# Gate and up of the feed-forward: half the contraction by seven block products, down products between the blocks, hidden tile turned through memory

## The chip, the cores and the metric

One core of a Trainium2 chip runs the whole program. The metric is the device time of one launch in microseconds, the median of several runs. TensorE multiplies; VectorE, ScalarE and GpSimd do the elementwise work; SyncE issues the loads of the weights.

## The reference

Two transformer layers over 256 tokens of width 2048, in float32. The mixers (sparse and linear attention in layer 0, stick-breaking attention in layer 1) are not touched. Each layer has this feed-forward, with `w_gate` and `w_up` of 2048 x 5632 and `w_down` of 5632 x 2048:

```python
xn = rmsnorm(h, norm_g)
h = h + (silu(xn @ w_gate) * (xn @ w_up)) @ w_down
```

## The kernel before

**Products.** The tokens stand in two halves of 128 (`tt`), the contraction in chunks of 128, the columns in blocks of 512. A float32 operand is split into a rounded part and a remainder (`hi`, `lo`), and a product is three passes of TensorE: hi x hi, hi x lo, lo x hi (L201 to L203). The activations, already turned and split, are `aH` and `aL` (`hH` and `hL` for the hidden tile); the row's norm factor is applied after the product.

**The stream of weights.** `unit` (L176) handles four chunks: SyncE loads 1 MB into a `raw` tile (two buffers), then for each half of two chunks ScalarE casts to `whi` (L99), VectorE subtracts to `wlo` (L100), four buffers each, and TensorE makes 2 chunks x 2 halves of tokens x 3 passes = 12 products of 512 columns. Such a half is called a half unit. `block` strings units together: 16 chunks are 8 half units, 96 products.

**The feed-forward.** The 11 blocks of hidden columns stand in groups of three (the last has two). `gate_up` makes a group: for each block the gate's 96 products, silu on ScalarE (L799), the up's 96 products, the multiplication on VectorE (L802), both halves into `sl`. Then `sl` is turned: 16 transposes on VectorE per block (L128), each turning 32 x 32 squares of a quarter of the partitions into `hx`, and a split into `hH`, `hL` (L789, L790). `down` multiplies a group's hidden tile with `w_down` in four column blocks and adds them to `h` (L234). The order is: gate and up of group 0, gate and up of group 1, all four column blocks of group 0's down, and so on.

**Order of the work.** The code is written out in one stream; the small tasks (turns, splits) wait in a list and are let in one at a time after a half unit (`later`, `tick`). A scheduler then gives every engine a fixed order, and an engine works through its order strictly, waiting where an operand is not there. A buffer is written again when its last reader is done. Products go to four PSUM tiles in turn (`mm`), transposes to four others (`at`).

Of the kernel before, what the change touches and what calls it, by code (L numbers as in the profile page):

```python
# [9 lines left out]
F32 = mybir.dt.float32  # L10
F32R = mybir.dt.float32r
# [6 lines left out]
NT = 2  # L18
# [9 lines left out]
def trunk_kernel(ctx: ExitStack, tc: tile.TileContext, x, p, even_norm, even_w_in, even_w_gk,  # L28
# [10 lines left out]
    psm = ctx.enter_context(tc.tile_pool(name="psm", bufs=4, space=bass.MemoryType.PSUM))  # L39
    pst = ctx.enter_context(tc.tile_pool(name="pst", bufs=4, space=bass.MemoryType.PSUM))  # L40

    def mm_tile():
        return psm.tile([P, NB], F32, name="mm")

    def at_tile():
        return pst.tile([P, NB], F32, name="at")

# [17 lines left out]
    # the activation tables and the tensor engine's clock are up when the data comes  # L65
# [7 lines left out]
    # norm gains, one row of 128 per chunk, turned so that a chunk's gains lie along the partitions  # L73
# [61 lines left out]
    def turn_h(dst, norm, c2):  # L135
        """Chunks 2*c2 and 2*c2+1 of h, transposed, times the gain, split."""
# [24 lines left out]
    def later(fn, key=None, delay=2, after=None):  # L161
        """fn, some half units of weights from now, and some after the work that `after` names."""
# [13 lines left out]
    def unit(ps, stat, k0, cols, first, last, nk=KU, kw0=None, step=KU, pre=None):  # L176
        """nk chunks of the contraction: cols = [(weight, first column, width)]."""
# [10 lines left out]
        for j in range(0, nk, 2):  # L188
# [794 lines left out]
```

## Time and profile before

| | |
|---|---|
| median of 3 runs | 2441.42 us (2440.93 to 2441.71) |
| the profiled execution, first to last instruction | 2438.5 us |
| TensorE, VectorE, ScalarE, GpSimd busy | 99%, 62%, 47%, 1% |
| first gate load of layer 0, last down load of layer 1 | 374.0 us, 2307.2 us |

The busy share of an engine is an average over stages. What a change is worth depends on which engine is late in its stage; for that the rows below show time lines of the feed-forward, where several engines can be laid side by side by their microseconds. A matmul's duration in the trace includes its way through the array; the distance between starts is what it costs in a stream.

### The profile page before, as it was taken

The page shows a single profiled execution, that of the slowest core. Times are in us where ns is not written, and L with a number is a line of the kernel's source. Part 1 is how long each engine was busy: PE and PEld are TensorE (multiplying, and loading weights), DVE is VectorE, ACT ScalarE, POOL GpSimd, SP SyncE. Part 2 cuts the span into 40 slices and gives each one's busy share as a digit, 9 for nine tenths or more (in the row PEclk, how much of TensorE's full clock was granted, in tenths as well). Part 3 has the DMA queues.
Part 4 walks back from the last instruction along what each step waited for, and adds up shares of the span by engine and source line. Part 5 has one row for each costly group of instructions (what it writes and reads, how often), then busy time and mean ns, then how long its engine had stood idle before and what let it go on. Part 6 is the DMA issues. An engine that isn't in the chain of part 4 may idle for free.

```text
span 2438.5 us, 27647 instructions
## 1 busy us (share of the span) xinstructions
PE 2417.6 (99%) x10966; PEld 1996.5 (82%) x10966; DVE 1506.6 (62%) x1907; ACT 1154.1 (47%) x1418; POOL 19.2 (1%) x45
## 2 busy tenths in 40 slices
PE   8999999999999999999999999999999999999998
PEld 7887788888888888888888888888888888888887
DVE  5765555766756665655676666557667556556564
ACT  6644444344434434446546565544444344444463
POOL 0000000000000000000000000000000000000000
PEclk9999999999999999999999999999999999999999
DMA  6454455566556565555554454555655655556563
GB/s 211 147 169 151 144 194 186 189 196 201 189 192 193 186 205 183 198 190 185 178 190 156 161 184 165 180 190 177 203 190 192 205 190 186 196 187 206 182 231 123
DMA packets 231651, 450.01 MB, mean 185 GB/s; under 512 B 9457, under 2 KB 16337, under 8 KB 231394
## 3 DMA queue, kind: packets, MB, share of 16 engines
q1 hardware_dynamic: 231234, 447.07, 55.6%
q8 instruction: 86, 1.41, 0.2%
q10 hardware_dynamic: 288, 1.18, 0.1%
q14 instruction: 43, 0.35, 0.0%
HBM read 446.12 MB, written 2.10 MB: 184 GB/s over the span
## 4 chain that ended last, share of the span: by engine, by line
PE 91%; issue 5%; ACT 2%; DVE 1%; DMA 1%; SPq 0%; POOLq 0%; POOL 0%; DVEq 0%; ACTq 0%
PE mm L202 29%; PE mm L201 29%; PE mm L203 29%; PE at L141 1%; DVE kT L128 1%; DVE wlo L100 0%; DMA raw<-in_odd_w_in_dram 0%; PE at L424 0%; DMA h<-in_x_dram 0%; PE at L742 0%; DVE sp L719 0%; ACT whi L99 0%; ACT sp L716 0%; ACT sp L715 0%; ACT L715 0%
## 5 line engine op out<-in xcount | busy, mean ns | idle before, releaser
L100 DVE TENSOR_TENSOR wlo<-raw,whi 128x1024 fp32r<-128x1024 f32 (+2 forms) x848 | 1020.7, 1213 | 794.1 <-ACT whi L99 790.1
L99 ACT CAST whi<-raw 128x1024 fp32r<-128x1024 f32 (+2 forms) x848 | 874.8, 1042 | 1053.5 <-PE mm L203 668.8
L201 PE MATMUL mm<-whi,aH 128*128 128x512 f32 (+2 forms) x2656 | 1036.9, 390 | 0.7 <-ACT whi L99 0.7
L202 PE MATMUL mm<-wlo,aH 128*128 128x512 f32 (+2 forms) x2656 | 1028.8, 387 | 4.1 <-DVE wlo L100 4.1
L203 PE MATMUL mm<-whi,aL 128*128 128x512 f32 (+2 forms) x2656 | 1028.7, 387 | 0.0
L202 PEld LDWEIGHTS mm<-wlo,aH 128*128 128x128 f32 x2656 | 499.4, 188 | 104.7 <-DVE wlo L100 5.9
L203 PEld LDWEIGHTS mm<-whi,aL 128*128 128x128 f32 x2656 | 499.1, 188 | 103.4 <-issue 1.0
L201 PEld LDWEIGHTS mm<-whi,aH 128*128 128x128 f32 x2656 | 499.2, 188 | 102.9 <-issue 2.8
L201 PE MATMUL mm<-whi,hH 128*128 128x512 f32 x704 | 277.2, 394 | 0.0
L202 PE MATMUL mm<-wlo,hH 128*128 128x512 f32 x704 | 277.0, 393 | 0.0
L203 PE MATMUL mm<-whi,hL 128*128 128x512 f32 x704 | 273.6, 389 | 0.0
L128 DVE STREAM_TRANSPOSE hx<-sl 32x256 f32<-32x256 f32 x352 | 153.6, 436 | 6.1
L201 PEld LDWEIGHTS mm<-whi,hH 128*128 128x128 f32 x704 | 132.2, 188 | 30.0
L203 PEld LDWEIGHTS mm<-whi,hL 128*128 128x128 f32 x704 | 132.2, 188 | 29.7
L202 PEld LDWEIGHTS mm<-wlo,hH 128*128 128x128 f32 x704 | 132.4, 188 | 26.1
L146 ACT ACTIVATE aH<-at,gT 128x256 fp32r<-128x256 f32 x96 | 45.1, 473 | 51.4 <-DVE aL L147 47.5
L789 ACT CAST hH<-hx 128x1024 fp32r<-128x1024 f32 x22 | 23.2, 1054 | 92.6 <-DVE hx L128 92.6
L147 DVE SCALAR_TENSOR_TENSOR aL<-at,gT,aH 128x256 fp32r<-128x256 f32 x96 | 45.8, 480 | 22.0 <-ACT aH L146 21.9
L234 DVE TENSOR_TENSOR h<-mm,h 128x512 f32<-128x512 f32 x80 | 52.4, 682 | 2.7 <-PE mm L203 2.7
L141 PE MATMUL at<-ident,h 128*128 128x128 f32 x192 | 30.5, 283 | 5.0 <-DMA h<-in_x_dram 5.0
L141 PEld LDWEIGHTS at<-ident,h 128*128 128x128 f32 x192 | 24.9, 145 | 11.8 <-DMA h<-in_x_dram 3.0
L128 DVE STREAM_TRANSPOSE qT<-tok 32x256 f32<-32x256 f32 x64 | 27.9, 436 | 6.8 <-ACT tok L762 5.8
(221 smaller groups left out, 806.8 us busy)
## 6 DMA issues: line engine op xcount, KB each, us to landing
raw<-in_ffn_w_gate_dram SPq DMA_DIRECT2D x88, 1024.0 KB, 5.2
raw<-in_ffn_w_up_dram SPq DMA_DIRECT2D x88, 1024.0 KB, 5.2
raw<-in_ffn_w_down_dram SPq DMA_DIRECT2D x88, 1024.0 KB, 5.0
raw<-in_odd_w_in_dram SPq DMA_DIRECT2D x48, 1024.0 KB, 5.2
raw<-in_even_w_in_dram SPq DMA_DIRECT2D x36, 1024.0 KB, 5.0
raw<-in_ple_w_gate_dram SPq DMA_DIRECT2D x28, 1024.0 KB, 5.1
raw<-in_even_w_out_dram SPq DMA_DIRECT2D x16, 1024.0 KB, 5.1
raw<-in_odd_w_out_dram SPq DMA_DIRECT2D x16, 1024.0 KB, 5.0
```

The source lines that it names most:

```text
L99: nc.scalar.copy(hi, raw)
L100: nc.vector.tensor_tensor(lo, raw, hi.bitcast(F32), OP.subtract)
L128: nc.vector.transpose(dst[32 * a:32 * a + 32, :, :, 32 * q:32 * q + 32], src.rearrange("p t (m a c) -> p t m a c", a=4, c=32)[32 * q:32 * ...
L141: nc.tensor.transpose(ps[:, c, tt, :], h[:, tt, k * P:(k + 1) * P], ident)
L146: nc.scalar.activation(dst[0][:, k, :], src, AF.Copy, scale=g)
L147: nc.vector.scalar_tensor_tensor(dst[1][:, k, :], src, g, dst[0][:, k, :].bitcast(F32), op0=OP.mult, op1=OP.subtract)
L201: nc.tensor.matmul(ps[tt][:, :n], sh, hi[:, c, :n], start=st, stop=False)
L202: nc.tensor.matmul(ps[tt][:, :n], sh, lo[:, c, :n], start=False, stop=False)
L203: nc.tensor.matmul(ps[tt][:, :n], sl, hi[:, c, :n], start=False, stop=en)
L234: nc.vector.tensor_tensor(hs, ps[tt], hs, OP.add)
L789: nc.scalar.copy(d[0], t)
```

## The change

**Seven products for eight.** Take two chunks of the contraction, the two halves of the tokens, and one block of 512 columns of gate beside the same of up: a 2 x 2 block matrix times a 2 x 2 block matrix, eight block products, each of three passes. The change makes seven products of sums (Winograd's form) from them and combines the seven results. It does so for the first eight of the 16 chunks (four *pairs*), in blocks 1 to 10; the other eight chunks go through `unit` as before (here called the plain units, four half units of gate and four of up). Block 0 stays as it was.

The sums of activations are made and split once a layer, in block 0 (`sums_of_operand`, into `sT`). The sums of weights are made on VectorE in every pair (L850 to L852, into `T`): one of 1024 elements per partition and two of 512. A pair's split goes in four pieces with 1, 2, 2 and 2 blocks of 512 columns, thus 3, 6, 6 and 6 products. The seven results lie in PSUM banks that are fixed by number; the plain units are added on top of four of them, and VectorE and ScalarE combine the banks (L876 to L880, L886) in the tile `E`. All PSUM is now one tile `bank` whose slices are handed out in turn.

**Down between the blocks.** After each block of gate and up in groups 1 to 3, one or two of the four column blocks of the group before follow.

**The turn through memory.** In place of 16 transposes and `hx`, one transpose of 32 x 32 squares over all partitions (L143), four stores to DRAM of 128 KB and two loads of 256 KB, all on GpSimd's queue (L147, L151). The cast (L904) and the subtraction (L905) of what comes back follow at least four half units later.

```diff
-    psm = ctx.enter_context(tc.tile_pool(name="psm", bufs=4, space=bass.MemoryType.PSUM))
-    pst = ctx.enter_context(tc.tile_pool(name="pst", bufs=4, space=bass.MemoryType.PSUM))
-
-    def mm_tile():
-        return psm.tile([P, NB], F32, name="mm")
-
-    def at_tile():
-        return pst.tile([P, NB], F32, name="at")
...
+    bank = psp.tile([P, 8, NB], F32, name="bank")
+    turns = {"mm": 0, "at": 0}
+
+    def mm_tile():
+        turns["mm"] += 1
+        return bank[:, (turns["mm"] - 1) % 4]
+
+    def at_tile():
+        turns["at"] += 1
+        return bank[:, 4 + (turns["at"] - 1) % 4]
...
+    def cross(src, pool):
+
+
+
+        tq = pool.tile([P, 4, NT, 4, 32], F32, name="tq", bufs=1)
+        nc.vector.transpose(tq.rearrange("p a t m r -> p t m a r"),
+                            src.rearrange("p t (m a c) -> p t m a c", a=4, c=32))
+        y = yp.tile([4, 32, 4, NT, P], F32, name="ty")
+        for q in range(4):
+            nc.gpsimd.dma_start(y[:, :, q].rearrange("a c t n -> c a (t n)"),
+                                tq[32 * q:32 * q + 32].rearrange("c a t m r -> c a (t m r)"))
+        x = pool.tile([P, NT, 4, 4, 32], F32, name="tx", bufs=1)
+        for t in range(NT):
+            nc.gpsimd.dma_start(x[:, t].rearrange("p q m r -> p q (m r)"),
+                                y[:, :, :, t].rearrange("a c q n -> (a c) q n"))
+        return x.rearrange("p t q m r -> p m (t q) r")
+
...
-                    st = first and j + c == 0
+                    st = first and tt >= begun and j + c == 0
...
+    NS = 4
+    B2, B4, B3, B22, B1, B5, B6, B7 = range(8)
+
...
+        ST = act.tile([P, 2, 4, NS, P], F32R, name="sT", tag="aH")
+        work = act.tile([P, 8, NB], F32, name="work", tag="aL")
+        T, E = work[:, 0:4], work[:, 4:8]
...
+        def product(p, stat, hi, lo, first, last):
+            for m, (a, b) in enumerate(((stat[0], hi), (stat[0], lo), (stat[1], hi))):
+                nc.tensor.matmul(bank[:, p], a, b, start=first and m == 0, stop=last and m == 2)
+
+        def pair(j, b):
+
+            raw = wp.tile([P, KU, NB], F32, name="raw", bufs=2).rearrange("p (r c) n -> p r c n", r=2)
+            for c, w in enumerate((ffn_w_gate[i], ffn_w_up[i])):
+                nc.sync.dma_start(raw[:, :, c], w[2 * j * P:(2 * j + 2) * P, b * NB:(b + 1) * NB]
+                                  .rearrange("(k q) n -> q k n", q=P))
+
+            nc.vector.tensor_tensor(T[:, 0:2], raw[:, 0], raw[:, :, 1], OP.add)
+            nc.vector.tensor_tensor(T[:, 2], T[:, 1], raw[:, 0, 0], OP.add)
+            nc.vector.tensor_tensor(T[:, 3], T[:, 2], raw[:, 1, 0], OP.add)
+
+            def tok(c, t):
+                return [x[:, 2 * j + c, t * P:(t + 1) * P] for x in xs]
+
+            def comb(n):
+                return [ST[:, hl, n, j] for hl in range(2)]
+
+            pieces = [(raw[:, 0, 0:1], [(B1, tok(0, 0))]), (T[:, 0:2], [(B5, comb(0)), (B7, comb(2))]),
+                      (T[:, 2:4], [(B6, comb(1)), (B4, tok(1, 1))]),
+                      (raw[:, 1], [(B2, tok(1, 0)), (B3, comb(3))])]
+            for n, (src, ps) in enumerate(pieces):
+                hi = wp.tile([P, 2, NB], F32R, name="whi")
+                lo = wp.tile([P, 2, NB], F32R, name="wlo")
+                split_sb(src, hi[:, :len(ps)], lo[:, :len(ps)])
+                for c, (p, stat) in enumerate(ps):
+                    product(p, stat, hi[:, c], lo[:, c], j == 0, j == NS - 1 and p >= B1)
+                if n % 2:
+                    tick()
+
+        def gate_up_7(b):
+            need(("sT", i))
+            for j in range(NS):
+                pair(j, b)
+            nc.scalar.copy(E[:, 0], bank[:, B1])
+            nc.vector.tensor_tensor(E[:, 2], bank[:, B6], E[:, 0], OP.add)
+            nc.vector.tensor_tensor(E[:, 1], bank[:, B7], E[:, 2], OP.add)
+            nc.vector.tensor_tensor(E[:, 3], bank[:, B5], E[:, 1], OP.subtract)
+            nc.vector.tensor_tensor(E[:, 2], bank[:, B5], E[:, 2], OP.subtract)
+            for n, w in enumerate((ffn_w_gate[i], ffn_w_up[i])):
+                for k in range(2 * NS, KC, KU):
+                    unit([bank[:, 2 * n], bank[:, 2 * n + 1]], xs, k, [(w, b * NB, NB)], n == 1 and k == 2 * NS,
+                         k + KU == KC, begun=1)
+                e = E[:, 2 * n:2 * n + 2]
+                nc.vector.tensor_tensor(e, bank[:, 2 * n:2 * n + 2], e, OP.add)
+                if n == 0:
+                    sl = fp.tile([P, NT, NB], F32, name="sl")
+                    for tt in range(NT):
+                        nc.scalar.activation(sl[:, tt], E[:, tt], AF.Silu, scale=rstd_of(nkey)[:, tt:tt + 1])
+            return sl, [E[:, 2 + tt] for tt in range(NT)]
+
+        def gate_up_8(b):
...
+            later(sums_of_operand, key=("sT", i))
+            return sl, block(xs, [(ffn_w_up[i], b * NB, NB)])
...
+            x = {}
+            later(lambda: x.update(x=cross(sl, fp)), key=("xT", i, b))
+            later(lambda: split_hid(hT[gi], x["x"], 4 * n), key=("hT", i, b), after=(("xT", i, b), 4))
...
+        for gi, g in enumerate(groups):
+            for n in range(len(g)):
+                gate_up(gi, n)
+                if gi:
+                    for cb in range(4 * n // len(g), 4 * (n + 1) // len(g)):
+                        down(gi - 1, cb, None)
+        nx = nx_fn()
+        for cb in range(4):
+            down(len(groups) - 1, cb, nx)
+        return nx
```

The order on VectorE before, in layer 0 behind a block of gate and up (L802 multiplies gate and up, L128 turns, L100 subtracts for the weights, L790 for the hidden tile):

```order
L802 SCALAR_TENSOR_TENSOR sl<-mm,rstd,sl 128x512 x2
L128 STREAM_TRANSPOSE hx<-sl 32x2x4x32 x8
L100 TENSOR_TENSOR wlo<-raw,whi 128x1024
L128 STREAM_TRANSPOSE hx<-sl 32x2x4x32 x4
L100 TENSOR_TENSOR wlo<-raw,whi 128x1024
L128 STREAM_TRANSPOSE hx<-sl 32x2x4x32 x4
L100 TENSOR_TENSOR wlo<-raw,whi 128x1024
L790 TENSOR_TENSOR hL<-hx,hH 128x1024
L100 TENSOR_TENSOR wlo<-raw,whi 128x1024 x13
```

And of the change, in block 4 from the end of the column block of down products that stands before it (L259 adds to `h`, L850 to L852 sum weights, L107 subtracts for the weights, L905 for the hidden tile):

```order
L259 TENSOR_TENSOR h<-bank,h 128x512 x2
L851 TENSOR_TENSOR work<-work,raw 128x512
L107 TENSOR_TENSOR wlo<-raw,whi 128x1024
L905 TENSOR_TENSOR hL<-tx,hH 128x1024
L852 TENSOR_TENSOR work<-work,raw 128x512
L107 TENSOR_TENSOR wlo<-raw,whi 128x512
L107 TENSOR_TENSOR wlo<-work,whi 128x1024 x2
L107 TENSOR_TENSOR wlo<-raw,whi 128x1024
L850 TENSOR_TENSOR work<-raw 128x1024
L107 TENSOR_TENSOR wlo<-raw,whi 128x512
L851 TENSOR_TENSOR work<-work,raw 128x512
L107 TENSOR_TENSOR wlo<-work,whi 128x1024
```

Where VectorE had one subtraction per 12 products, it now has a sum or two beside each subtraction per 6 products.

The order on ScalarE before, over a block of gate and up in layer 0 (L799 is silu, L99 casts weights, L789 the hidden tile):

```order
L799 ACTIVATE sl<-mm,rstd 128x512 x2
L99 CAST whi<-raw 128x1024 x11
L789 CAST hH<-hx 128x1024
L99 CAST whi<-raw 128x1024 x5
L799 ACTIVATE sl<-mm,rstd 128x512 x2
L99 CAST whi<-raw 128x1024 x11
```

And of the change, in the last two pairs of block 4 and behind them (L106 casts weights, L876 copies a PSUM bank to `E`, L890 is silu):

```order
L106 CAST whi<-raw 128x512
L106 CAST whi<-work 128x1024 x2
L106 CAST whi<-raw 128x1024
L106 CAST whi<-raw 128x512
L106 CAST whi<-work 128x1024
L876 COPY work<-bank 128x512
L106 CAST whi<-work 128x1024
L106 CAST whi<-raw 128x1024 x8
L890 ACTIVATE sl<-work,rstd 128x512 x2
```

The copy L876 stands between the casts of the last pair's second and third piece.

## Rows read from the trace of the kernel before

**Rows 1.** The page: span, busy time of each engine, slices of TensorE, VectorE and clock.
```profile
span 2438.5 us, 27647 instructions
...
PE 2417.6 (99%) x10966; PEld 1996.5 (82%) x10966; DVE 1506.6 (62%) x1907; ACT 1154.1 (47%) x1418; POOL 19.2 (1%) x45
...
PE   8999999999999999999999999999999999999998
...
DVE  5765555766756665655676666557667556556564
...
PEclk9999999999999999999999999999999999999999
```

**Rows 2.** Busy time by stretches of the first feed-forward.
```profile
core 0: us, PE busy (x) PEld busy (x) DVE busy (x) ACT busy (x) POOL busy (x), PEclk, DMA share, GB/s
...
580.00:680.00 100.00, 100.00 (x442) 82.58 (x441) 65.03 (x78) 43.48 (x44) 0.00 (x0) 1.00 0.61 202
680.00:780.00 100.00, 100.00 (x441) 82.52 (x440) 56.60 (x62) 39.87 (x39) 0.00 (x0) 1.00 0.58 188
780.00:880.00 100.00, 100.00 (x441) 82.58 (x440) 65.87 (x79) 42.53 (x43) 0.00 (x0) 1.00 0.60 195
```

**Rows 3.** Timeline of ScalarE in the first feed-forward: start, duration, instruction, idle before.
```profile
765.92 1.06 ACT L99 CAST whi<-raw 128x1024 fp32r<-128x1024 f32 x1 [1.66 <-PE mm L203]
...
777.69 2.00 ACT L99 CAST whi<-raw 128x1024 fp32r<-128x1024 f32 x2 [3.54 <-DMA raw<-in_ffn_w_up_dram]
```

**Rows 4.** Timeline of VectorE over the same microseconds.
```profile
759.99 1.40 DVE L802 SCALAR_TENSOR_TENSOR sl<-mm,rstd,sl 128x512 f32<-128x512 f32 x2
761.43 3.57 DVE L128 STREAM_TRANSPOSE hx<-sl 32x256 f32<-32x256 f32 x8
...
771.20 1.23 DVE L100 TENSOR_TENSOR wlo<-raw,whi 128x1024 fp32r<-128x1024 f32 x1
772.34 1.22 DVE L790 TENSOR_TENSOR hL<-hx,hH 128x1024 fp32r<-128x1024 f32 x1
773.48 2.35 DVE L100 TENSOR_TENSOR wlo<-raw,whi 128x1024 fp32r<-128x1024 f32 x2
```

**Rows 5.** SyncE's queue in the same microseconds, two answers.
```profile
772.45 3.77 SPq L184 DMA_DIRECT2D raw<-in_ffn_w_up_dram  x2
...
775.85 0.37 SPq L184 DMA_DIRECT2D raw<-in_ffn_w_up_dram  x1
```

**Rows 6.** DMA issues: KB each, median us from issue to landing.
```profile
raw<-in_ffn_w_gate_dram SPq DMA_DIRECT2D x88, 1024.0 KB, 5.2
...
raw<-in_ple_w_gate_dram SPq DMA_DIRECT2D x4, 512.0 KB, 3.6
...
out_dram<-h SPq DMA_DIRECT2D x8, 256.0 KB, 2.8
...
praw<-in_p_dram SPq DMA_DIRECT2D x2, 256.0 KB, 5.1
```

**Rows 7.** VectorE by line and shape: count, busy us, mean ns, idle before.
```profile
L100 DVE TENSOR_TENSOR wlo<-raw,whi 128x1024 fp32r<-128x1024 f32 x832 | 1010.4, 1223 | 779.8 <-ACT whi L99 775.9
L128 DVE STREAM_TRANSPOSE hx<-sl 32x256 f32<-32x256 f32 x352 | 153.6, 436 | 6.1
...
L867 DVE TENSOR_TENSOR h<-h,sgm 128x512 f32<-128x512 f32 x14 | 9.0, 685 | 0.0
...
L100 DVE TENSOR_TENSOR wlo<-raw,whi 128x512 fp32r<-128x512 f32 x8 | 5.3, 688 | 6.1 <-ACT whi L99 6.0
```

**Rows 8.** Timeline of VectorE: two additions to h.
```profile
716.44 1.28 DVE L234 TENSOR_TENSOR h<-mm,h 128x512 f32<-128x512 f32 x2
```

**Rows 9.** Timeline of ScalarE: two copies out of PSUM.
```profile
1115.84 1.05 ACT L856 COPY pe<-mm 128x512 f32<-128x512 f32 x2
```

**Rows 10.** Busy time and clock of the first 20 us (columns as in Rows 2).
```profile
0.00:20.00 20.00, 13.36 (x55) 10.85 (x56) 8.10 (x13) 10.79 (x23) 3.96 (x24) 1.00 0.81 274
```

More of the change, by code (lines that the diff above doesn't have):

```diff
@@ L174, in tick, with unit @@
                 run_fill()
-    def unit(ps, stat, k0, cols, first, last, nk=KU, kw0=None, step=KU, pre=None):
+    def unit(ps, stat, k0, cols, first, last, nk=KU, kw0=None, step=KU, pre=None, begun=0):
         kw0 = k0 if kw0 is None else kw0
@@ L809, in down, with sums_of_operand @@
-        def down(gi, nx):
+        ST = act.tile([P, 2, 4, NS, P], F32R, name="sT", tag="aH")
+        work = act.tile([P, 8, NB], F32, name="work", tag="aL")
+        T, E = work[:, 0:4], work[:, 4:8]
+        def sums_of_operand():
+            a = T.rearrange("p a n -> p (a n)").rearrange("p (j c t q) -> p j c t q", c=2, t=NT, q=P)
+            nc.vector.tensor_tensor(T.rearrange("p a n -> p (a n)"),
+                                    xs[0][:, :2 * NS].rearrange("p k n -> p (k n)").bitcast(F32),
+                                    xs[1][:, :2 * NS].rearrange("p k n -> p (k n)").bitcast(F32), OP.add)
+            s = E.rearrange("p a (j q) -> p a j q", q=P)
+            nc.vector.tensor_tensor(s[:, 0], a[:, :, 0, 1], a[:, :, 1, 1], OP.subtract)
+            nc.vector.tensor_tensor(s[:, 1], s[:, 0], a[:, :, 0, 0], OP.subtract)
+            nc.vector.tensor_tensor(s[:, 2], a[:, :, 0, 0], a[:, :, 0, 1], OP.subtract)
+            nc.vector.tensor_tensor(s[:, 3], s[:, 1], a[:, :, 1, 0], OP.add)
+            for n in range(2):
+                split_sb(s[:, 2 * n:2 * n + 2], ST[:, 0, 2 * n:2 * n + 2], ST[:, 1, 2 * n:2 * n + 2])
@@ new lines, in gate_up_8, with split_hid @@
+        def gate_up_8(b):
+            pg = block(xs, [(ffn_w_gate[i], b * NB, NB)], key=nkey)
+            rs = rstd_of(nkey)
+            sl = fp.tile([P, NT, NB], F32, name="sl")
+            for tt in range(NT):
+                nc.scalar.activation(sl[:, tt], pg[tt], AF.Silu, scale=rs[:, tt:tt + 1])
+            later(sums_of_operand, key=("sT", i))
+            return sl, block(xs, [(ffn_w_up[i], b * NB, NB)])
+        def split_hid(dst, x, k0):
+            d = [dst[n][:, k0:k0 + 4, :].rearrange("p m (q r) -> p m q r", q=8) for n in range(2)]
+            nc.scalar.copy(d[0], x)
+            nc.vector.tensor_tensor(d[1], x, d[0].bitcast(F32), OP.subtract)
@@ new lines, in gate_up @@
+        def gate_up(gi, n):
+            b = groups[gi][n]
+            if n == 0:
+                hT[gi] = (fp.tile([P, 12, NT * P], F32R, name="hH"), fp.tile([P, 12, NT * P], F32R, name="hL"))
+            sl, pu = gate_up_7(b) if b else gate_up_8(b)
+            rs = rstd_of(nkey)
+            for tt in range(NT):
+                nc.vector.scalar_tensor_tensor(sl[:, tt], pu[tt], rs[:, tt:tt + 1], sl[:, tt], op0=OP.mult,
+                                               op1=OP.mult)
+            x = {}
+            later(lambda: x.update(x=cross(sl, fp)), key=("xT", i, b))
+            later(lambda: split_hid(hT[gi], x["x"], 4 * n), key=("hT", i, b), after=(("xT", i, b), 4))
@@ L810, in down @@
+        def down(gi, cb, nx):
             for b in groups[gi]:
@@ L812, in down @@
             nk = 4 * len(groups[gi])
-            for cb in range(4):
-                ps = block(hT[gi], [(ffn_w_down[i], cb * NB, NB)], nk=nk, kw=groups[gi][0] * 4)
-                add_to_h(ps, cb)
-                if nx:
-                    finish_cols(nx, cb)
-        gate_up(0)
-        for gi in range(1, len(groups)):
-            gate_up(gi)
-            down(gi - 1, None)
+            ps = block(hT[gi], [(ffn_w_down[i], cb * NB, NB)], nk=nk, kw=groups[gi][0] * 4)
+            add_to_h(ps, cb)
+            if nx:
+                finish_cols(nx, cb)
+        for gi, g in enumerate(groups):
[4 more added lines that the diff above has]
+                        down(gi - 1, cb, None)
         nx = nx_fn()
-        down(len(groups) - 1, nx)
+        for cb in range(4):
+            down(len(groups) - 1, cb, nx)
         return nx
```

22 lines of the change are left out of this document (2 added, 20 removed).

## The prediction

> **What bounds the kernel now.** The page's busy shares come first: TensorE is busy for 99% of the span, VectorE for 62%, ScalarE for 47%, GpSimd for 1%, and the granted clock is in its top tenth in every slice [rows 1]. Next, the stretches of the feed-forward: each 100 us hold 441 products, TensorE has no gap, the clock is 1.00 (2.4 GHz), and VectorE is busy for 57 to 66 us of the 100 [rows 2]. One product of 512 columns therefore takes 100 / 441 = 0.2267 us, a half unit of 12 takes 2.72 us. So the kernel is bound by the count of products, and taking products away pays as long as their operands come in time.
>
> How they come is read from the engines' own time lines. ScalarE's rounding cast waits 1.66 us for the last product that reads one of the four `whi` buffers [rows 3]. So the pair ScalarE and VectorE is three pieces ahead of TensorE and no more: one buffer is being read, three are filled. That is the whole reserve when VectorE gets more to do than TensorE does. The weights come with little reserve too: a subtraction that began at 771.20 freed a buffer at 772.43 [rows 4], SyncE issued the next load at 772.45 [rows 5], and the cast that needed it began at 777.69 [rows 3], 5.26 us after the release. The median load of 1 MB lands in 5.2 us [rows 6], beside 5.44 us of products for the same tile.
>
> **What goes.** The first of eleven blocks in each layer stays as it is. In the other ten the four pairs of chunks take 4 x 21 = 84 products where there were 96, so 12 x 10 x 2 = 240 go: 240 x 0.2267 = 54.4 us. The 352 small transposes (153.6 us on VectorE) [rows 7] go as well, for 22 large ones; since TensorE never waited there [rows 2], they give back no time by themselves.
>
> **What VectorE gets in a pair.** Long operations (1024 per partition) last 1.22 us, but two in a row take 2.35 us, so each costs 1.13 [rows 4]. Short ones (512) last 0.69 [rows 7], and two in a row take 1.28 us, so each costs 0.60 [rows 8]. The sums of weights are not in the trace of before; the nearest rows are the subtraction `wlo` (both operands in SBUF, same size) and the addition `h<-h,sgm` (685 ns, float32 from SBUF) [rows 7]. If ends and starts did not overlap they would cost 1.22 and 0.69. I take 1.13 and 0.60, because the overlap is seen wherever VectorE runs without waiting. A pair is then one long sum, two short sums, three long subtractions and one short: 4 x 1.13 + 3 x 0.60 = 6.32 us. TensorE needs 21 x 0.2267 = 4.76. Over a whole group of three blocks and its down products VectorE still has less to do than TensorE, but in the pairs it is the slower one, and its reserve is three pieces.
>
> **One window worked out.** I take the window from the end of the last product before the first pair (time zero) to the first product after the fourth pair, where TensorE needs 84 x 0.2267 = 19.04 us. Call a pair's four pieces A (short, 3 products), B, C, D (6 each). At zero A, B and C are ready and VectorE stands at the two additions to `h`, which wait for this last product. From there the listing of the change gives for blocks 4, 5, 7 and 8, which follow one column block of down products: two additions 1.20, a short sum 0.60, D 1.13, the remainder of the turned hidden tile (`hL`) 1.13, the rest of the second pair 0.60 + 0.60 + 3 x 1.13 = 4.59, two pairs 12.64, the first combination 0.60, and the first subtraction of the plain units 1.13, with 0.14 for its write and the handover (1.22 less 1.13, and some 0.05). Sum 23.2. Three waits lie between:
> - The last pair's sum needs its weights. Their buffer is freed by the second pair's D; from there VectorE has 3 x 0.60 + 2 x 1.13 = 4.06 us of other work, the load needs 5.26, and somewhat more for two issues of 0.37 us [rows 5]: 5.4, a wait of 1.3. If two half-size loads overlap wholly (3.6 us for 512 KB [rows 6]) it is nothing.
> - ScalarE's copy of the first product's bank stands between the last pair's casts of B and C. It needs the last A product: after A's subtraction 0.14 + 0.68 of products + 0.05 + 0.53 for the copy (two in a row take 1.05 [rows 9]) + 0.95 for the cast (two take 2.00 [rows 3]) + 0.1 = 2.45 us; VectorE has 0.60 + 1.13 to do, so it waits 0.7. A late D before it pushes this to 1.1, which I take.
> - The first combination needs the C products of the last pair: 0.4.
>
> That is 26.0 us where TensorE needs 19.04: 7.0 us of waiting in each of the four blocks. Blocks 6, 9 and 10, behind two column blocks, have no `hL` there (1.13 less), but the third pair then waits 0.8 for its weights: 25.7, 6.6 each. Block 1 follows the plain block: two products 1.30 (1.40 for two, less the overlap [rows 4]) and the large transpose in place of the additions. The transpose is 128 x 1024; by the small one (436 ns for 256 [rows 7]) it is between 1.2 (169 ns fixed and 1.04 ns an element) and 1.74 (four times); I take 1.24. It has no wait for the copy: 26.2, so 7.2. Blocks 2 and 3 follow a block directly, so that its last long addition, C, both products and the transpose all lie in the window: 28.5, so 9.5 each. A layer waits 4 x 7.0 + 3 x 6.6 + 7.2 + 2 x 9.5 = 74; both 148.
>
> **What is costed at nothing.** The combinations and additions of the plain units lie beside 8 half units (21.8 us of products against 17.4 us of VectorE). The operand sums in block 0 (about 7 us) lie beside 43 us of products with 18 us of subtractions. Outside the feed-forward VectorE's and ScalarE's rows stand as before. The turn through memory: the four stores and two loads must end before ScalarE's cast of the result. In blocks behind one column block VectorE ends the transpose 5.9 us after the last up product, and the cast is due after the 72 down products and D's cast: 16.3 + 1.0 - 5.9 = 11.4 us of cover. No GpSimd transfer is in the trace. The nearest rows are a 256 KB store, 2.8 us, and a 256 KB load, 5.1 us [rows 6]: 7.9 us if the stores overlap and the loads do, 21.4 if all six queue. I take 7.9 with six issues of 0.4, 10.3, since loads on SyncE's queue overlap; it fits, with 1 us to spare.
>
> **The sum.** 2438.5 - 54.4 + 148 = 2532 of span; the median shown is 2.9 us above the span, so 2535 us. By the bounds: no wait for weights or for the copy leaves 4 x 4.1 + 3 x 3.0 + 5.5 + 2 x 7.7 = 46 per layer, 93 in all, and 2480 us; operations without overlap add 2.3 us to each of 20 windows, 2581 us.
>
> **Rivals.**
> - The load evens out (faster). A block is 42.7 us of VectorE (four pairs 25.3, the plain units and what follows them 17.4), the four column blocks of down products 31.9; three blocks with them are 160 us, against 188 of TensorE. If the reserve carried the pairs, nothing but 54.4 us would change: 2387. It decides at the point where the reserve reaches what VectorE lacks in a window: 23.2 - 19.0 = 4.1 us at least, after the three pieces are counted. The wait for the fourth buffer speaks against it [rows 3]. 6%.
> - The turn comes late (slower still). ScalarE's cast then holds all casts behind it. At 16 us it is 4.6 us late in four blocks of a layer and some 2 in three others, 25 per layer: 2585. At 21.4 us it is 10 late in seven: 2675. For it: six dependent transfers, 128 to 512 pieces each, on a queue that no row shows. Against: the cover of 11.4. 18%.
>
>   The Trainium skill has a rule for this on the page SBUF — State Buffer, section "SBUF: two separate sides": descriptors of a GpSimd transfer are written through a port that VectorE locks in its two-port modes, so such a transfer starves under a busy VectorE. The rows show none of these modes in the pairs, since 1024 float32 take 1.13 us, about one element a cycle. By the page DMA: Bandwidth & Descriptors, section "Anatomy of one DMA — SWDGE (gpsimd) path" (2.0 us plus the bytes at 436 GB/s) the estimate is 4.9 us overlapped and 14.4 in a queue, so the sum would stay or grow by some 30 us.
> - The clock falls to 1.2 GHz in the windows, where TensorE would be busy about 73%: 84 products at 0.43 us are 36 us, 10 more in each of 20 windows, 2735. Against: the first 20 us, with 13.4 busy, had 1.00 [rows 10]. 3%.
>
> **How the numbers follow.** The forecast has 70%, its own range 2480 to 2581. The late turn has 18%, evening out 6%, the clock 3%, the rest 3%. From 2478 to 2605 I count the forecast and some half of the late turn, 8 in 10. About 0.2% (5 us) is what a measurement of this kernel can tell from no change. Faster 0.06, within 0.02, slower 0.92.
>
> **What would show it.** TensorE: 240 products fewer, gaps of 1 to 3 us that end on `wlo` in the pairs and nearly none in the plain units and down products; the clock 1.00. VectorE: almost no idle time in the pairs, the sums at 1.22 and 0.69 us. The weight sums of the last pair wait for loads; the cast of the turned tile waits for nothing. It would be wrong if TensorE stayed closed in the pairs, or if the gaps ended on the turned tile.

## The result, and the profile after

The changed kernel takes 2558.1 us (2554.6 to 2563.4, 4 runs) against 2441.2 us (2440.1 to 2441.7, 4 runs): 1.048 times as long, 95% interval 1.0465 to 1.0495. The forecast was 2535, the range 2478 to 2605. The page of the changed kernel, against [rows 1]:

```profile
span 2556.7 us, 28206 instructions
...
PE 2437.1 (95%) x10726; PEld 1936.1 (76%) x10726; DVE 1804.7 (71%) x2111; ACT 1285.2 (50%) x1602; POOL 101.5 (4%) x177
```

240 products are gone (10966 to 10726). If nothing else had changed, the span would be 2438.5 - 54.4 = 2384.1; it is 2556.7, so TensorE waits 172.6 us more. Three stretches of the feed-forward, columns as in [rows 2], show it: products per 100 us fall from 442 to between 343 and 392, while VectorE does 75 to 84 us of work in place of 57 to 66 [rows 2].

```profile
480.00:580.00 100.00, 87.73 (x343) 64.32 (x342) 84.07 (x89) 49.75 (x56) 7.40 (x12) 0.97 0.55 182
580.00:680.00 100.00, 93.84 (x392) 71.56 (x390) 80.44 (x85) 45.66 (x50) 7.39 (x12) 1.00 0.58 194
680.00:780.00 100.00, 91.90 (x385) 70.56 (x385) 75.47 (x80) 47.16 (x51) 3.69 (x6) 1.00 0.58 189
```

What TensorE waits for (line, what released it; us in total, times, longest):

```profile
PE bank L841 <- DVE wlo L107: 48.8, 79, 1.5
PE bank L841 <- ACT whi L106: 23.6, 51, 1.0
PE bank L226 <- DVE work L886: 16.9, 12, 1.4
PE bank L227 <- DVE wlo L107: 8.9, 26, 0.8
```

The first two rows are the pairs' products (L841) waiting for their splits, as forecast. The third is new: the first product of a down column waits for L886, VectorE's last addition over the banks that this product is to write. The fourth is in 20 of its 26 places, with 4.4 us, a plain unit after the pairs; the other six lie outside the feed-forward, where the kernel before has five such waits too. These sums come short of 172.6, for three reasons that the time line shows: a product's modelled duration is 0.39 us where starts are 0.23 apart, so each wait is shown about 0.16 us too short; one shorter than 0.15 us is not shown; and in five short stretches at half clock 35 products start 0.43 us apart, 7 us more in all.

The window can be measured as it was forecast. In block 5 the last down product starts at 666.39, the pairs' first at 666.62, and the plain units' first at 693.63:

```profile
666.39 0.39 PE L228 MATMUL bank<-whi,hL 128*128 128x512 f32 x1
666.62 0.39 PE L841 MATMUL bank<-whi,aH 128*128 128x512 f32 x1
...
693.63 0.62 PE L226 MATMUL bank<-whi,aH 128*128 128x512 f32 x2
```

That is 27.0 us for products of 19.04, so 8.0 us of waiting. Read in the same way (where one product of the plain units stands inside, 0.23 us is taken off):

| block | 1 | 2 | 3 | 4 | 5 | 6 | 7 | 8 | 9 | 10 | sum |
|---|---|---|---|---|---|---|---|---|---|---|---|
| forecast | 7.2 | 9.5 | 9.5 | 7.0 | 7.0 | 6.6 | 7.0 | 7.0 | 6.6 | 6.6 | 74 |
| layer 0 | 5.7 | 10.8 | 9.9 | 5.9 | 8.0 | 4.5 | 5.7 | 8.1 | 3.9 | 4.0 | 66 |
| layer 1 | 6.6 | 9.7 | 10.3 | 6.1 | 8.5 | 3.8 | 5.7 | 9.5 | 4.2 | 3.9 | 68 |

So the windows hold 135 us of the 172.6, and 38 lie outside them. The forecast's window ends with the first subtraction of the plain units. The measured one ends with their first product, which needs only the cast; the products that wait for that subtraction, in all some 6 us, are therefore among the 38. VectorE is busy for 93% of the 20 windows.

VectorE and SyncE in block 5, against [rows 4] and [rows 5]: the second pair's last split frees a raw buffer at 677.00, both halves are asked for at 677.03 and 677.45 (the second issue takes 1.11 us), and the last pair's sum starts at 683.09, after a wait.

```profile
675.79 1.21 DVE L107 TENSOR_TENSOR wlo<-raw,whi 128x1024 fp32r<-128x1024 f32 x1
...
683.09 1.23 DVE L850 TENSOR_TENSOR work<-raw 128x1024 f32<-128x1024 f32 x1 [1.93 <-DMA raw<-in_ffn_w_up_dram]
```
```profile
677.03 0.37 SPq L847 DMA_DIRECT2D raw<-in_ffn_w_gate_dram  x1
677.45 1.11 SPq L847 DMA_DIRECT2D raw<-in_ffn_w_up_dram  x1
```

The operations of VectorE that no row of before showed (against [rows 7]; count, busy us, mean ns), and the transfers, against [rows 6]:

```profile
L850 DVE TENSOR_TENSOR work<-raw 128x1024 f32<-128x1024 f32 x80 | 97.8, 1222 | 42.6 <-DMA raw<-in_ffn_w_up_dram 42.3
L852 DVE TENSOR_TENSOR work<-work,raw 128x512 f32<-128x512 f32 x80 | 54.8, 685 | 0.8
...
L143 DVE STREAM_TRANSPOSE tq<-sl 128x1024 f32<-128x1024 f32 x22 | 27.2, 1238 | 0.0
```
```profile
raw<-in_ffn_w_gate_dram SPq DMA_DIRECT2D x80, 512.0 KB, 3.9
raw<-in_ffn_w_up_dram SPq DMA_DIRECT2D x80, 512.0 KB, 4.7
ty<-tq POOLq DMA_DIRECT2D x88, 128.0 KB, 4.1
tx<-ty POOLq DMA_DIRECT2D x44, 256.0 KB, 4.3
```

The turn through memory of block 0, on GpSimd's queue, and all of ScalarE's waits for it. The stores are issued from 437.86, the loads from 443.39; the second load is issued 0.76 us later and lands 3.9 us after that, at 448.0.

```profile
437.86 2.40 POOL L147 DMA_DIRECT2D ty<-tq  x4 [41.86 <-issue]
443.39 1.51 POOL L151 DMA_DIRECT2D tx<-ty  x2 [3.13 <-DMA ty<-tq]
```
```profile
ACT hH L904 <- DMA tx<-ty: 5.5, 6, 1.6
```

### The profile page after: what moved, and what is told of

Same layout as the page of the kernel before. It is cut to its first block, busy times and chain, and to the rows that moved or that the text cites. A ratio compares the mean times of both kernels' runs of the same rounds, so it can differ in the third digit from the quotient of the medians.

```text
span 2556.7 us, 28206 instructions
## 1 busy us (share of the span) xinstructions
PE 2437.1 (95%) x10726; PEld 1936.1 (76%) x10726; DVE 1804.7 (71%) x2111; ACT 1285.2 (50%) x1602; POOL 101.5 (4%) x177
## 4 chain that ended last, share of the span: by engine, by line
PE 57%; DVE 17%; DMA 13%; issue 7%; ACT 5%; SPq 0%; DVEq 0%; ACTq 0%; POOLq 0%; POOL 0%
PE bank L227 18%; PE bank L228 18%; PE bank L226 17%; DVE wlo L107 9%; DMA raw<-in_ffn_w_up_dram 7%; DMA raw<-in_ffn_w_gate_dram 4%; ACT whi L106 3%; DVE work L850 2%; PE bank L841 1%; DVE work L851 1%; PE bank L165 1%; DVE kT L135 1%; DVE work L886 1%; DVE work L852 1%; DVE hL L905 1%
## 5 line engine op out<-in xcount | busy, mean ns | idle before, releaser
L107 DVE TENSOR_TENSOR wlo<-raw,whi 128x1024 fp32r<-128x1024 f32 (+2 forms) x848 | 974.3, 1160 | 504.2 <-ACT whi L106 502.1
L106 ACT CAST whi<-raw 128x1024 fp32r<-128x1024 f32 (+2 forms) x848 | 830.6, 1000 | 868.6 <-PE bank L228 373.9
L227 PE MATMUL bank<-wlo,aH 128*128 128x512 f32 (+2 forms) x2016 | 784.6, 389 | 10.4 <-DVE wlo L107 8.9
L226 PE MATMUL bank<-whi,aH 128*128 128x512 f32 (+2 forms) x2016 | 784.1, 391 | 1.5 <-ACT whi L106 1.5
L228 PE MATMUL bank<-whi,aL 128*128 128x512 f32 (+2 forms) x2016 | 780.6, 387 | 0.0
L227 PEld LDWEIGHTS bank<-wlo,aH 128*128 128x128 f32 x2016 | 379.2, 188 | 102.0 <-DVE wlo L107 28.8
L226 PEld LDWEIGHTS bank<-whi,aH 128*128 128x128 f32 x2016 | 379.1, 188 | 80.4 <-ACT whi L106 3.7
L228 PEld LDWEIGHTS bank<-whi,aL 128*128 128x128 f32 x2016 | 379.0, 188 | 77.2 <-issue 1.0
L226 PE MATMUL bank<-whi,hH 128*128 128x512 f32 x704 | 276.4, 393 | 16.9 <-DVE work L886 16.9
L106 ACT CAST whi<-work 128x1024 fp32r<-128x1024 f32 x160 | 167.9, 1049 | 237.4 <-DVE work L852 106.1
L228 PE MATMUL bank<-whi,hL 128*128 128x512 f32 x704 | 276.5, 393 | 0.0
L227 PE MATMUL bank<-wlo,hH 128*128 128x512 f32 x704 | 275.9, 392 | 0.0
L841 PE MATMUL bank<-whi,sT 128*128 128x512 f32 x640 | 242.3, 407 | 20.5 <-ACT whi L106 19.1
L107 DVE TENSOR_TENSOR wlo<-work,whi 128x1024 fp32r<-128x1024 f32 x160 | 193.5, 1221 | 22.1 <-ACT whi L106 21.6
L226 PEld LDWEIGHTS bank<-whi,hH 128*128 128x128 f32 x704 | 132.2, 188 | 50.0 <-ACT whi L106 19.8
L841 PEld LDWEIGHTS bank<-whi,sT 128*128 128x128 f32 x640 | 120.2, 190 | 62.8 <-ACT whi L106 41.4
L841 PE MATMUL bank<-wlo,sT 128*128 128x512 f32 x320 | 133.2, 416 | 24.0 <-DVE wlo L107 24.0
L227 PEld LDWEIGHTS bank<-wlo,hH 128*128 128x128 f32 x704 | 132.2, 188 | 29.0
L850 DVE TENSOR_TENSOR work<-raw 128x1024 f32<-128x1024 f32 x80 | 97.8, 1222 | 42.6 <-DMA raw<-in_ffn_w_up_dram 42.3
L841 PE MATMUL bank<-wlo,aH 128*128 128x512 f32 x240 | 100.8, 420 | 24.7 <-DVE wlo L107 24.7
L841 PEld LDWEIGHTS bank<-wlo,sT 128*128 128x128 f32 x320 | 61.3, 192 | 55.8 <-DVE wlo L107 42.8
```

The lines of the kernel that those rows point to most:

```text
L106: nc.scalar.copy(hi, raw)
L107: nc.vector.tensor_tensor(lo, raw, hi.bitcast(F32), OP.subtract)
L226: nc.tensor.matmul(ps[tt][:, :n], sh, hi[:, c, :n], start=st, stop=False)
L227: nc.tensor.matmul(ps[tt][:, :n], sh, lo[:, c, :n], start=False, stop=False)
L228: nc.tensor.matmul(ps[tt][:, :n], sl, hi[:, c, :n], start=False, stop=en)
L841: nc.tensor.matmul(bank[:, p], a, b, start=first and m == 0, stop=last and m == 2)
```

## The experiments

The theory: VectorE's weight sums, and loads behind them, make a pair longer than its products. Its rivals: the other parts of the change (turn, order, banks), the clock. Every ratio is to the kernel before, measured beside it. The number 2387 below is 2441.2 less 54.4.

**1. The sums of weights left out.** The pieces that were sums take raw weights.

```diff
-            nc.vector.tensor_tensor(T[:, 0:2], raw[:, 0], raw[:, :, 1], OP.add)
-            nc.vector.tensor_tensor(T[:, 2], T[:, 1], raw[:, 0, 0], OP.add)
-            nc.vector.tensor_tensor(T[:, 3], T[:, 2], raw[:, 1, 0], OP.add)
...
```

> The three sums of weights of every pair are left out (the pieces are cast from the loaded weights as they are), so gate and up are not what the reference wants; products, loads, pieces, turn and order stay. Theory (VectorE has more to do than TensorE in the pairs): a pair is 3.99 us of VectorE instead of 6.32, below TensorE's 4.76, so nearly all waiting in the pairs goes: 2395 to 2430 us. Rival (the turn through memory holds ScalarE or the queues): about 2555, nothing moves. Rival (the loads of the pairs alone): 2510 or more, since the loads are the same.

2461.1 us, ratio 1.0081 (1.0054 to 1.0108). Without the three sums 97 us go, the largest single part. But 74 us over 2387 stay, more than the theory gave.

**2. Eight products in all blocks**, turn, order of down and the one PSUM tile as in the changed kernel. Block 0's sums of activations are not made either.

```diff
-            sl, pu = gate_up_7(b) if b else gate_up_8(b)
+            sl, pu = gate_up_8(b)
...
```

> All eleven blocks of a layer by eight products, as block 0; down products between the blocks, the turn through memory and the fixed PSUM banks stay. Theory (the pairs on VectorE): 2436 to 2450 us, as before the change. Rival (the turn through memory, or the order of down products, costs the time): 2500 or more.

2440.1 us, ratio 0.9996 (0.9987 to 1.0006), as expected. Turn and order of down cost nothing as long as the pairs are not there. The fixed banks and the combinations are not in this kernel.

**3. The old turn under seven products.** The 16 small transposes a block in place of the trip through memory.

```diff
-            later(lambda: x.update(x=cross(sl, fp)), key=("xT", i, b))
+            for a in range(4):
+                later(lambda d=hx, t=sl, a=a: turn_blocks(d.rearrange("p m (t c) -> p t m c", t=NT), t, a))
...
```

> Seven products stay, the hidden tile is turned by 16 small transposes on VectorE as before the change. Theory: VectorE gets 7.1 us instead of 1.24 per block, of which 4 to 8 transposes (1.8 to 3.6 us) and more fall into the windows of the pairs, nothing is gained: 2580 to 2660 us. Rival (the turn through memory costs the time): 2450 to 2500.

2620.7 us, ratio 1.0732 (1.0716 to 1.0748), as expected. The turn through memory, worth nothing in experiment 2, is worth 62 us here: VectorE's time has a price only where VectorE is late.

**4. Half of the pairs' loads.**

```diff
-            for c, w in enumerate((ffn_w_gate[i], ffn_w_up[i])):
-                nc.sync.dma_start(raw[:, :, c], w[...])
+            nc.sync.dma_start(raw, ffn_w_gate[i][...])
```

> In the pairs only the gate's half of the weights is loaded (512 KB instead of 2 x 512 KB) and stands for the up's half too, so the values are not the reference's; VectorE, ScalarE and TensorE do the same instructions. Theory: the waits of the weight sums for loads go (some 2 us in each of 20 windows, somewhat more by what they push): 2500 to 2530 us, still far above before. Rival (the loads alone make the waiting): 2440 or less. Rival (the turn): 2555.

2532.1 us, ratio 1.0371 (1.0355 to 1.0386): 26 us less than the changed kernel, 2 us above the range that was expected.

**5. Neither sums nor second half.** Experiments 1 and 4 together.

> Left out: the three sums of weights of every pair (two of its products take the raw weights instead) and the load of the up half (the gate half stands for it). The seven products, the order of down, the fixed banks and the turn through memory stay. Theory (the pairs are slower than their products because of VectorE's sums and, behind them, of the loads into two raw buffers; together they are all of the lost time but some 25 us, which TensorE waits for the bank that VectorE still reads): 2441 less 54 is 2387, and with 0 to 30 us of that wait 2387 to 2420. Rival (something else in the changed program loses time too: the order in which the splits of hi and lo follow each other on ScalarE and VectorE, or TensorE's clock): 2430 to 2465, near the kernel without the sums (2461).

2446.5 us, ratio 1.0027 (1.0016 to 1.0038). Sums and loads are 112 of the lost time together; 60 us over 2387 remain, and the theory's bound (2420) is passed. What TensorE waits for in this kernel:

```profile
PE bank L226 <- DVE work L880: 22.7, 12, 2.8
PE bank L227 <- DVE wlo L107: 12.6, 26, 1.5
PE bank L226 <- ACT whi L106: 6.3, 6, 1.6
```

Hardly a pair waits (L841 has 0.2 us in all). The 12 waits for the read bank (L880 is L886 of the changed kernel) are 22.7 us. Of the 32 at L226 and L227 in units, eight with 5.9 us lie outside the feed-forward; the other 24, with 13.0 us, are in the first units after the pairs. These 36 waits are 35.7 us, and 41.5 with 0.16 us more for each. So a third and a fourth cost lie outside the pairs; what is left of the 60 us was not taken apart.

**6. Pairs spread.** The same work, in another order: pair, gate unit, pair, up unit, twice. The combinations of the banks stand before the last up unit.

```diff
+            for j, (n, k) in enumerate(((0, 8), (1, 8), (0, 12), (1, 12))):
+                pair(j, b)
...
+                plain(n, k)
```

> Nothing left out; only the order in a block changes: pair, gate unit, pair, up unit, pair, gate unit, pair, up unit, where the four pairs came first. Theory (VectorE falls behind only because four pairs stand in a row: 6.32 us of VectorE against 4.76 us of TensorE each; a pair and a plain unit together are 6.32 + 2.26 = 8.6 us of VectorE against 4.76 + 5.44 = 10.2 us of TensorE, and 2 MB of weights are asked for in 10.2 us instead of 1 MB in 4.76): most of the 172 us of waiting goes, and 54 us of products stay gone: 2390 to 2440. Rival 1 (VectorE's work in a block as a whole, with the down column between, is what binds, wherever it stands): 2470 to 2520. Rival 2 (loads of a pair in two halves are late wherever the pair stands): 2450 to 2490, with the raw tiles ending VectorE's waits.

2528.7 us, ratio 1.0358 (1.0343 to 1.0374): 29 us better than the changed kernel, where the theory had 118 or more. VectorE's time line shows a period: the sum starts at 608.18, 619.33 and 630.59, every 11.2 us where the products take 10.2.

```profile
608.18 1.22 DVE L850 TENSOR_TENSOR work<-raw 128x1024 f32<-128x1024 f32 x1
...
613.19 3.49 DVE L107 TENSOR_TENSOR wlo<-raw,whi 128x1024 fp32r<-128x1024 f32 x3
618.69 0.69 DVE L107 TENSOR_TENSOR wlo<-raw,whi 128x512 fp32r<-128x512 f32 x1 [2.01 <-ACT whi L106]
619.33 1.23 DVE L850 TENSOR_TENSOR work<-raw 128x1024 f32<-128x1024 f32 x1
```
```profile
614.43 0.37 SPq L847 DMA_DIRECT2D raw<-in_ffn_w_gate_dram  x1
```
```profile
618.03 0.62 ACT L106 CAST whi<-raw 128x512 fp32r<-128x512 f32 x1 [3.18 <-DMA raw<-in_ffn_w_gate_dram]
```

VectorE is idle for 2.0 us of each round, so it is not short of time. The first of the three L107 at 613.19 is the pair's last split; it frees the raw tile at about 614.4, the load goes out at 614.43, and the cast can start at 618.03, 3.6 us later. With two raw tiles and strict alternation the pairs always have the same one: held for some 7.5 us, loaded for 3.6. Rival 2 of the expectation names the place, though not the size: the time lies above every range that was given.

**7. Two of the sums on GpSimd**, on top of 6.

```diff
-            nc.vector.tensor_tensor(T[:, 2], T[:, 1], raw[:, 0, 0], OP.add)
+            nc.gpsimd.tensor_tensor(T[:, 2], T[:, 1], raw[:, 0, 0], OP.add)
...
```

> Nothing left out: the spread order, and the two short sums of every pair (1.2 us of VectorE) on GpSimd, where a sum of 512 took 1.29 us in the kernel before. Theory (after the spreading VectorE is no longer what binds): the same as the spread order within 15 us, 2390 to 2440; the sums are later by 2 x 0.65 us in a chain that has slack. Rival 1 (VectorE still binds after the spreading): faster than the spread order by 20 to 60 us. Rival 2 (VectorE and GpSimd hold each other up, as the Trainium skill's page SBUF — State Buffer, section SUBTLE: VectorE ↔ GpSimd shared port, would let one fear): slower than the spread order by 20 us or more, with VectorE's or GpSimd's own durations longer than 1.22 and 1.29 us.

2663.0 us, ratio 1.0912 (1.0894 to 1.0930): 134 us worse. GpSimd, and VectorE at the same time:

```profile
613.20 1.30 POOL L851 TENSOR_TENSOR work<-work,raw 128x512 f32<-128x512 f32 x1 [6.94 <-DVE work L850]
614.58 2.16 POOL L852 TENSOR_TENSOR work<-work,raw 128x512 f32<-128x512 f32 x1
```
```profile
614.26 1.32 DVE L107 TENSOR_TENSOR wlo<-work,whi 128x1024 fp32r<-128x1024 f32 x1 [1.20 <-ACT whi L106]
```

The first sum lasts 1.30 us; the second starts inside VectorE's subtraction and ends 1.16 us after it, and the subtraction, which started inside the first sum, lasts 1.32 in place of 1.22. The Trainium skill, page SBUF — State Buffer, section "SBUF: two separate sides" (the expectation gives a heading that the page does not have), says that a VectorE operation with two SBUF inputs and a GpSimd operation that reads SBUF exclude each other for a whole instruction; these rows agree. The raw tile is held longer by the two slow sums, and the period, 11.2 us in experiment 6, becomes 14.6 us here (613.20 to the next L851 at 627.82, with the additions to `h` and `hL` in between) and some 13.4 in the two rounds behind it.

**8. Two pairs per block**, spread.

> Nothing left out: only two pairs (a quarter of the contraction) of each block by seven products, each behind other units: pair, gate, up, gate, pair, up, gate, up. 120 products go instead of 240: 120 x 0.2267 = 27.2 us. Theory (a lone pair among plain units is carried by the three pieces that are split ahead): 2441 - 27 = 2414, with some waits 2410 to 2425. Rival 1 (the spread order of four pairs has no waits left either): then this one is slower than that by up to 27 us, which the comparison of the two shows. Rival 2 (each pair costs waiting of its own wherever it stands): 2430 to 2470.

2482.5 us, ratio 1.0167 (1.0152 to 1.0182), above every range that was given. In 580 to 680 us TensorE has no gap (440 products), so two pairs are carried there. The largest part of the loss lies at the starts of down, and it is more than the wait. The wait, TensorE's time line at two such starts, and its clock (busy, clock, DMA share, GB/s):

```profile
PE bank L226 <- DVE work L882: 27.4, 12, 3.1
```
```profile
573.08 0.47 PE L226 MATMUL bank<-whi,hH 128*128 128x512 f32 x1 [2.71 <-DVE work L882]
...
574.06 0.63 PE L226 MATMUL bank<-whi,hH 128*128 128x512 f32 x1
574.49 0.63 PE L227 MATMUL bank<-wlo,hH 128*128 128x512 f32 x1
...
1052.36 0.47 PE L226 MATMUL bank<-whi,hH 128*128 128x512 f32 x1 [2.65 <-DVE work L882]
1052.67 0.39 PE L227 MATMUL bank<-wlo,hH 128*128 128x512 f32 x1
```
```profile
574.00:576.00 2.00, 2.00 (x6) 0.50 0.50 103
...
1053.00:1055.00 2.00, 2.00 (x11) 1.00 0.29 34
```

At 573.08, after 2.71 us without a product, the granted clock falls to 0.50 (1.2 GHz) and products start 0.43 us apart instead of 0.23. At 1052.36, after 2.65 us, it stays at 1.00. Five of this run's 12 waits for L882 were followed by a stretch at 0.50, one of them of 1.93 us (at 774.38); seven were not. In experiment 5 a wait of 2.79 us (at 684.90) was not. So the length of the wait by itself does not tell whether the clock falls, and what does is left open.

**9. Free banks for down**, in the changed kernel.

```diff
+                    turns["mm"] = 0
                     for cb in range(4 * n // len(g), 4 * (n + 1) // len(g)):
...
```

> Nothing left out; the changed kernel, only that the first column block of down behind a block takes banks 0 and 1, and not, in six of ten cases, banks 2 and 3, which VectorE's last addition over memory banks (L886) still reads. Theory (this wait of down's first product, 16.9 us in 12 places of the profile and about 0.16 us more in each that the modelled ends hide, is time lost for good, with some products at the lower clock behind it): 2558 less 19 to 35, 2523 to 2540, and the wait gone from the list. Rival (the time comes back: with down's products earlier, the next pairs find VectorE that much more behind): 2548 to 2562.

2543.5 us, ratio 1.0416 (1.0401 to 1.0432): 14.6 us, between the two expectations. The wait is gone; a part comes back in the pairs (L841 for `wlo`: 48.8 to 53.2 us).

**10. Spread, raw tile given back earlier, free banks.** The piece from the second raw half is split second, not last; down takes banks 6 and 7 last. In this run and the next the two products of that piece have each other's weights, gate's for up's; the work is the same in kind and count.

```diff
+            pieces = [(raw[:, 0, 0:1], [(B1, tok(0, 0))]), (raw[:, 1], [(B3, comb(3)), (B2, tok(1, 0))]),
+                      (T[:, 0:2], [(B5, comb(0)), (B7, comb(2))]), (T[:, 2:4], [(B6, comb(1)), (B4, tok(1, 1))])]
...
```

> Nothing left out: the spread order, with two things more. The pair's second raw half is split second instead of last, so that the raw buffer is given back two long splits (2.3 us) earlier; and down writes into banks that nothing reads any more. Theory (in the spread order a pair and its unit took 11.15 us against 10.2 us of products, because the one buffer that the pairs share is held 7.4 us and then loaded for 3.7; now 7.4 - 2.3 + 3.7 = 8.8 us): the waits at L841 go, and the bank wait with its slow products: 2395 to 2440. Rival (VectorE's work of a whole block, some 43 us against 41 us of products where no column of down stands between, binds): 2450 to 2500.

2432.8 us, ratio 0.9969 (0.9957 to 0.9980): 96 us better than experiment 6, as the theory had it, and under the kernel before. TensorE's waits in this kernel:

```profile
PE bank L841 <- DVE wlo L107: 9.2, 9, 2.6
PE bank L226 <- DVE work L881: 7.2, 8, 1.6
PE bank L841 <- ACT whi L106: 7.0, 9, 1.2
```

The waits of L841 for splits fall from 53 (31.5 and 21.5 in experiment 6) to 16 us, those for the bank that VectorE reads from 23.4 to 7.2. How the 96 us divide between the earlier return and the free banks was not tried. What is left lies mostly in blocks 1 and 2, which no down column follows: 392 products in 480 to 580 us, 426 to 438 in the later stretches.

**11. The same with two pairs.**

> Nothing left out: two pairs per block (half of the seven-product work), spread, with the early return of the raw buffer and down's free banks. Theory (of the 69 us that the two pairs stood above 2441 - 27 = 2414, the bank wait, 27.4 us in 12 places of up to 3.1 us, and the products at half clock behind each of them are nearly all): 2412 to 2432, faster than before. Rival (the pairs lose as much in other waits): 2445 to 2480. If four pairs bring no waits either, the four are faster than the two by up to 27 us.

2430.0 us, ratio 0.9961 (0.9949 to 0.9973), as expected. That is 52 us better than experiment 8; of the 27.4 us that were shown on VectorE's last addition there, 2.3 are left. The earlier return has a part in this too, which was not taken apart.

**12. The version that follows.** As 10, with the weights in their places, seven products from block 3 on, down in banks 6, 7 and 5, 3.

```diff
-            sl, pu = gate_up_7(b) if b else gate_up_8(b)
+            sl, pu = gate_up_7(b) if b > 2 else gate_up_8(b)
...
```

> Nothing left out. The spread order with the early return of the raw buffer (the two products of the second piece each with their own weights, which the last two runs had exchanged), but seven products only from block 3 on, behind which a column of down always stands; blocks 0 to 2 by eight; the columns of down in banks 6, 7 and then 5, 3, which nobody reads any more. 8 blocks x 2 layers x 12 x 0.2267 = 43.5 us of products go: 2441 - 43.5 = 2397. Theory (in the spread order with four pairs, 15 of the 24 us that a layer still lost lay in blocks 1 and 2, 380 to 580 us, where VectorE's block is longer than the products; the 9 us of the other blocks stay, or less with the bank waits gone): 2405 to 2420, faster than every kernel so far. Rival (the loss is one of every change from down to pairs and back, so it stays): 2425 to 2440.

2402.2 us (2401.4 to 2403.7), ratio 0.9843 (0.9830 to 0.9857): faster than both kernels, 3 us below the expected range, and 38.5 us of the 43.5 us of products are kept. The busy times, one stretch, and the pairs' largest wait:

```profile
PE 2377.6 (99%) x10774; PEld 1958.9 (82%) x10774; DVE 1712.3 (71%) x2007; ACT 1265.5 (53%) x1566; POOL 102.6 (4%) x177
```
```profile
580.00:680.00 100.00, 99.81 (x437) 81.34 (x436) 89.92 (x94) 56.10 (x61) 3.70 (x6) 1.00 0.66 218
```
```profile
PE bank L841 <- DVE wlo L107: 3.1, 6, 0.8
```

VectorE is busier in this stretch (90%) than in any stretch of the changed kernel shown above, and TensorE hardly waits.

## Why the prediction was right, and where its sizes were off

- **The products gone**: 240, as counted. Experiment 2 shows that the turn and the order of down do not move the time by themselves.
- **VectorE's operations**: 1222 and 685 ns against 1.22 and 0.69; the transpose 1238 ns against 1.24. Back to back they cost 1.13 and 0.60, as taken.
- **The pair is longer on VectorE than on TensorE**: shown. Without the sums 97 us go (experiment 1), the stretches of [rows 2] that were closed have gaps which end on the splits, and in the windows VectorE is busy for 93% of the time.
- **The windows**: 148 forecast, 135 measured. Blocks behind one column are as forecast on average (7.0 against 7.2), those behind two are not: 6.6 against 4.0. The trace shows what is missing there: VectorE waits for no load in those six windows, where the forecast had 1.3 for the last pair and 0.8 for the third. Behind one column it is not all right either: in blocks 5 and 8 VectorE reaches the additions to `h` 1.6 to 3.0 us after time zero, not at zero, since it had waited for a load just before. These four windows wait 8.5 us on average, those of blocks 4 and 7 only 5.9, so the agreement of the mean is partly luck. The windows with the longest waiting (blocks 2 and 3 of both layers, block 8 of layer 1) are also the ones in which the clock falls; in the first four it is not shown which comes first.
- **ScalarE's copy** between the last pair's casts: 1.1 us forecast in 14 windows. VectorE's wait behind it is 0.65 in seven of the eight behind one column and 1.17 in the six behind two; in block 8 of layer 1 it is 2.1, where products at half clock stand before the copy. That is 14 us where the forecast had 15.
- **The load of the last pair**: 5.4 us from release to use forecast, 6.1 in block 5, and the wait was 1.9 there, not 1.3. The forecast had 1.3 in each of 20 windows and 0.8 more in six, some 31. VectorE's waits at L850 are 42.3 us, of which only 20 lie inside the windows. Experiment 4 gives the loads 26 us of time. So they are of the right order, but not where they were forecast.
- **The turn through memory**: 10.3 us forecast from the first issue to the last landing. The first block of each layer took 10.2, but these are the shortest of 22 trips: the median is 11.7, above the cover of 11.4 that the forecast had behind one column block, and the longest 14.4. Still ScalarE waits for it only 5.5 us in the whole program, so the rival of the late turn is refuted. For a starving under VectorE the rows have no sign: the four issues and two dependent steps of 4.1 and 4.3 us fill most of the time.
- **The step that failed: "What is costed at nothing", the combinations beside the plain units.** It counted VectorE's sum (17.4 of 21.8 us) and took that as cover, but some of these operations have someone waiting behind them. The last addition (L886) holds the bank that down writes next: 16.9 us shown in 12 places, 18.8 by the distance of starts, worth 14.6 by itself (experiment 9). And the first units after the pairs wait for their splits: 4.4 us shown at L227, but 16 by the distance of starts with the product behind each, since these waits are shown too short or not at all; some 6 of the 16 belong to the first subtraction, which the forecast had in its window. Together these are 35 of the 38 us outside the windows, and with 13 too much inside them they make the difference of 25 us between 148 and 173. That the two errors go against each other is luck.
- **Evening out** (2387, chance 6%) was rightly small for this order, but the reason was only half of it. Its working said that VectorE has 160 us for 188 of TensorE over a group. In experiment 6 spreading alone did not reach it; experiments 10 and 12 show that the sum does carry where the order lets it, once the raw tile is given back in time and down takes free banks: 2402 with seven products in eight of eleven blocks.
- **The clock**: 0.97 in one stretch, down to 0.73 over 490 to 495 us. The sum had nothing for it and the rival 200; it took 7 us, so the rival did not come true.

Left open: how much of the 26 us of loads is the raw tile's holding, in the order with four pairs in a row; a third raw tile was not tried.

## What to carry to other kernels

A busy share that fits says little: between two engines stand a few buffers, and each has a loop of holding and loading whose length must be below the products' time; work such loops out one by one, then reorder for the earliest release before moving work to another engine. When results stay in fixed PSUM banks, ask who reads each bank last and who writes it next. And spread a stage that is short of one engine among stages that are not.

## What the runs showed of the hardware

- In experiment 8 a wait of 2.71 us in an otherwise closed stream of products was followed by eight starts 0.43 us apart, at a granted clock of 0.50: 3.4 us for 1.8, so 1.6 us on top of the wait. One of 1.93 us was followed by such a stretch too, and one of 2.65 us in the same run was not.
- In experiment 7 a GpSimd sum of 512 elements took 1.32 us on average as the first of two, and 2.08 us as the second, which starts beside VectorE's subtraction; that subtraction went from 1.22 to 1.28.
- On SyncE's queue the first issue of a pair's two loads took 0.37 us each time in the changed kernel; the second, with the first load under way, took 0.46 in the median and between 0.37 and 1.44.
